# Moving operands laid out in eight places of a row and read in pieces of four, in a fused decoder layer

## The chip, the cores and the metric

The kernel runs on one core of one Trainium2 chip, in one launch. The metric is the device time of that core in microseconds, from the first to the last instruction of the execution; lower is better. Three runs of the kernel before gave 1671.35 to 1672.09 us, median 1671.76 us. Engines are named as the profile names them: PE (TensorE, products), PEld (its weight loads), DVE (VectorE), ACT (ScalarE), POOL (GpSimd) and SP (the queue that issues most transfers).

## The reference

One step of a hybrid decoder layer over 320 tokens: 256 prompt tokens and 8 sequences of 8 sample tokens, which share all weights. Everything is float32.

```
xn = rms_norm(x, g_mix);  z = xn @ w_in                    # 2048 -> 8704 columns
b, c, h, q, k, v, gate_c, gate_a = split(z)
y_conv = (b * conv3(c * h)) @ w_conv_out                   # causal, width 3
attn   = window_attend(q, k, v, bias, sinks)               # 16 heads, 4 kv heads, window 128
y_attn = attn @ w_attn_out
h1 = x + (sigmoid(gate_c)*y_conv + sigmoid(gate_a)*y_attn) @ w_o
h2 = h1 + (silu(n @ w_gate) * (n @ w_up)) @ w_down         # n = rms_norm(h1, g_ffn), 5632 wide
y  = rms_norm(h2, g_final)                                 # also new k, v and conv state
```

## The kernel before

Activations lie with features on the partitions and the 320 tokens (`T`) along the row, 16 rows of 128 features (`KC`). To keep float32 accuracy with the quick `float32r` product, every operand is split into a rounded part "hi" and a rest "lo", and each product is made three times: hi weights by hi tokens, hi weights by lo tokens, lo weights by hi tokens. The weights are the stationary operand (128x128); the tokens are the moving operand, one contiguous row of 320 elements, and they are written to the first 320 columns of a PSUM bank of 512.

`product` (lines 128 to 151) makes two output blocks of 128 columns at a time. `load_cols` (98) brings 4 rows of 256 weight columns (512 KB) by SP, ACT rounds them (`whi`, line 95), DVE subtracts (`wlo`, line 96), and 24 matmuls use them at line 142; a product over 2048 features has 96 matmuls. `passes` writes out the order: hi-hi and hi-lo of one place, with the lo-weight products three behind. `kv_product` (307) is the same with four blocks (line 331). The stages in time are `kv`; `q`; four rounds of `C`, `H`, `B` with the attention as side work between their products; eight rounds of `gc`, `ga`, `yc`, `ya`; eight of `wo`; and then twice the gate and up products (`fg`, `fu`) and the down product (`dn`), for 28 and for 16 of the 44 rows of the feed-forward width (`FH`).

Who writes the moving operands, each a hi tile and a lo tile with rows of 320: `x_prep` (272) the normed input, line 789 the convolution's output `cv`, `prompt_pv` (555) and line 690 the attention's output `at`, line 831 the merged `m`, line 849 the feed-forward input `hh`/`hl`. `q2` (444) lends rows of `at` to the queries before the attention's output is there.

`down` (874) differs. A row of `a_t` has 640 elements: hi of tokens 0 to 319, lo of tokens 128 to 319, lo of tokens 0 to 127. One matmul takes 512 of them at once with hi weights (line 898: all hi, and lo of the last 192 tokens), so that a full bank is written; a second (902) has the 128 lo elements as its stationary operand and 512 weight columns as the moving one; a third (906) is lo weights by the 320 hi elements. DVE adds the bank's two parts to `hT` (915, 916). The last 512 output columns (lines 1016 to 1092) hold their weights in spare room, use 384 columns at line 1045, 320 at 1049, and finish the first 128 tokens row by row at line 1083, where tokens are stationary.

Few lines carry the layout:

```
ps[c][:, :T], w[:, k, c * P:(c + 1) * P], x(kc),                                   # 143, moving operand x(kc)
ps[c], parts[k][0][:, cs], a_t[:, k, 0:512], start=k == 0, stop=False              # 899
last["hi"] = nc.scalar.activation(a_t[:, f, 0:T], gs[c], AF.Copy)                  # 955
for t0, t1, d0 in ((P, T, T), (0, P, 512)):                                        # 956, two subtractions
```

Of the kernel before, what the change touches and what calls it, by code (L numbers as in the profile page):

```python
# [38 lines left out]
TR = T - P  # L39
XB = [1] * 4 + [2] * 6  # L40
# [4 lines left out]
def hybrid_layer(ctx: ExitStack, tc: tile.TileContext, a: dict, o: list):  # L45
# [40 lines left out]
    def raw_tile():  # L86
        return wp.tile([P, KT, CW], F32, tag="wraw", name=u("wraw"), bufs=4)

# [39 lines left out]
    def product(load, nk, xh, xl, name, tiles=None, loaded=None):  # L128

        ps = [ps_acc(u(name)) for _ in range(2)]  # L130
        k0 = 0
        for n in tiles or [min(KT, nk - k) for k in range(0, nk, KT)]:
            hi, lo = load(k0, n)
            if loaded:
                loaded()
            order = [(k, c) for k in range(n) for c in range(2)]
            if k0 + n == nk:
                order.sort(key=lambda kc: kc[1])
            for k, c, i in passes(order, k0 + n == nk):
                kc = k0 + k  # L140
                w, x = ((hi, xh), (hi, xl), (lo, xh))[i]
                last["mm"] = nc.tensor.matmul(  # L142
                    ps[c][:, :T], w[:, k, c * P:(c + 1) * P], x(kc),
                    start=(kc == 0 and i == 0), stop=(kc == nk - 1 and i == 2),
                )
# [70 lines left out]
    xh_t = xp.tile([P, KC, T], F32R, tag="xh", name="xh_t")  # L216
    xl_t = xp.tile([P, KC, T], F32R, tag="xl", name="xl_t")
# [6 lines left out]

    def xh(kc):
        return xh_t[:, kc, :]

    def xl(kc):
        return xl_t[:, kc, :]
# [42 lines left out]
    def x_prep(kc):  # L272
        if kc == 0:
            m1 = nc.vector.tensor_scalar(xh_t[:, kc, :], hT[:, kc, :], g_mix[:, kc:kc + 1], None, op0=ALU.mult)
        else:
            m1 = nc.scalar.activation(xh_t[:, kc, :], hT[:, kc, :], AF.Copy, scale=g_mix[:, kc:kc + 1])
        m2 = nc.vector.scalar_tensor_tensor(
            xl_t[:, kc, :], hT[:, kc, :], g_mix[:, kc:kc + 1], xh_t[:, kc, :].bitcast(F32),
            op0=ALU.mult, op1=ALU.subtract,
        )  # L280
        mark[kc] = (m1, m2)
# [25 lines left out]
    def kv_product(tiles, x_after):  # L307

        ps = [ps_acc(u("kv")) for _ in range(4)]
        k0 = 0  # L310
        x_prep(0)
        for i, n in enumerate(tiles):
            hi, lo = load_kv(k0, n)
            if i == 0:
                x_prep(1)
            for b in x_after.get(i, ()):
                x_load(b)
            order = [(k, c) for k in range(n) for c in range(4)]
            if k0 + n == KC:
                order.sort(key=lambda kc: kc[1])  # L320
            seq = passes(order, k0 + n == KC)
            if i == 0:
                seq.sort(key=lambda kcm: kcm[2])
            for k, c, m in seq:
                kc = k0 + k
                if k0 and (k, c, m) == (0, 3 if n > 1 else 1, 0) and k0 + n < KC:
                    for kk in range(tiles[i + 1]):
                        x_prep(k0 + n + kk)
                    tick()
                w, x = ((hi, xh), (hi, xl), (lo, xh))[m]  # L330
                last["mm"] = nc.tensor.matmul(  # L331
                    ps[c][:, :T], w[:, k, c * P:(c + 1) * P], x(kc),
                    start=(kc == 0 and m == 0), stop=(kc == KC - 1 and m == 2),
                )
            k0 += n
            if i == 0:
                tick()
        return ps
# [4 lines left out]
    def small_loads():  # L343

        behind = nc.gpsimd.tensor_copy(gate, xh_t[:, 7, 0:1].bitcast(F32))
# [77 lines left out]
    cv_h = yy.tile([P, 8, T], F32R, name="cv_h")  # L423
    cv_l = yy.tile([P, 8, T], F32R, name="cv_l")
    at_h = yy.tile([P, 8, T], F32R, name="at_h")
    at_l = yy.tile([P, 8, T], F32R, name="at_l")
# [17 lines left out]
    def q2(ch, par):  # L444
        return (at_h, at_l)[par][:, ch, 0:TP]
# [109 lines left out]
    def prompt_pv(j, gp, pts):  # L555
        po = ps_aux(u("po"))
        steps = ((0, 0, 0, True, True), (1, 0, 1, True, False), (1, 1, 2, False, True))
        for b, t, kb, st_, sp_ in steps:
            for par in range(2):
                kv = j * 2 + par  # L560
                nc.tensor.matmul(
                    po[par * 64:(par + 1) * 64, b * 256:(b + 1) * 256],
                    vn[t][:, kv * HD:(kv + 1) * HD], pts[par][:, kb, :], start=st_, stop=sp_,
                )
        src = po.rearrange("p (b g q) -> p g b q", b=2, g=2)
        ch = j * 4 + gp * 2
        dh = at_h[:, ch:ch + 2, 0:TP].rearrange("p g (b q) -> p g b q", b=2)
        dl = at_l[:, ch:ch + 2, 0:TP].rearrange("p g (b q) -> p g b q", b=2)
# [28 lines left out]
    def sample_attention(sm):  # L597
# [92 lines left out]
        for j in range(2):  # L690
            src = pos[j][:, 0:256].rearrange("p (b g t) -> p g b t", b=NB, g=GRP)
            dh = at_h[:, j * 4:j * 4 + 4, TP:T].rearrange("p g (b t) -> p g b t", b=NB)
            dl = at_l[:, j * 4:j * 4 + 4, TP:T].rearrange("p g (b t) -> p g b t", b=NB)
            nc.scalar.activation(dh, src, AF.Copy)
            nc.vector.tensor_sub(dl, src, dh.bitcast(F32))
# [49 lines left out]
    for cp in range(4):  # L745
# [34 lines left out]
        for c in range(2):  # L780
# [8 lines left out]
            split_to(cv_h[:, ch, :], cv_l[:, ch, :], t[:, :T])  # L789
# [8 lines left out]
    m_h = mm.tile([P, KC, T], F32R, name="m_h")  # L798
    m_l = mm.tile([P, KC, T], F32R, name="m_l")
# [8 lines left out]
    for mp in range(8):  # L808
        c0 = mp * CW
        sg = {}  # L810
        for nm, off, tag in (("gc", O_GC, "ta"), ("ga", O_GA, "tb")):
# [8 lines left out]
            lambda k: cv_h[:, k, :], lambda k: cv_l[:, k, :], "yc",  # L820
        )
        for c in range(2):
            nc.vector.tensor_mul(sg["gc", c], ps[c][:, :T], sg["gc", c])
        ps = product(
            lambda k0, n: load_cols(w_ao, k0, n, c0), 8, lambda k: at_h[:, k, :], lambda k: at_l[:, k, :], "ya",
        )
        for c in range(2):
# [3 lines left out]
            split_to(m_h[:, mp * 2 + c, :], m_l[:, mp * 2 + c, :], t)  # L831
# [6 lines left out]
    hh_t = xp.tile([P, KC, T], F32R, tag="xh", name="hh_t")  # L838
    hl_t = xp.tile([P, KC, T], F32R, tag="xl", name="hl_t")
    for mp in range(8):  # L840
# [3 lines left out]
            lambda k: m_h[:, k, :], lambda k: m_l[:, k, :], "wo",  # L844
        )
        for c in range(2):
            k = mp * 2 + c
            nc.vector.tensor_add(hT[:, k, :], ps[c][:, :T], hT[:, k, :])
            nc.scalar.activation(hh_t[:, k, :], hT[:, k, :], AF.Copy, scale=g_ffn[:, k:k + 1])
            nc.vector.scalar_tensor_tensor(  # L850
                hl_t[:, k, :], hT[:, k, :], g_ffn[:, k:k + 1], hh_t[:, k, :].bitcast(F32),
# [18 lines left out]
    FH = (28, 16)  # L870

    ylow = op.tile([P, E0], F32, name="ylow")

    def down(half, c0):
# [6 lines left out]
        for i, k0s in enumerate(sets):  # L881
# [13 lines left out]
            for k, c, m in passes(order, end):  # L895
                cs = slice(c * P, (c + 1) * P)
                if m == 0:
                    nc.tensor.matmul(  # L898
                        ps[c], parts[k][0][:, cs], a_t[:, k, 0:512], start=k == 0, stop=False
                    )  # L900
                elif m == 1 and c == 0:
                    nc.tensor.matmul(  # L902
                        low, a_t[:, k, 512:], parts[k][0], start=k == 0, stop=k == nf - 1 and c0 < E0
                    )
                elif m == 2:
                    last["mm"] = nc.tensor.matmul(  # L906
                        ps[c][:, :T], parts[k][1][:, cs], a_t[:, k, 0:T], start=False, stop=k == nf - 1
# [5 lines left out]
        for c in range(4):  # L913
            k = c0 // P + c
            nc.vector.tensor_add(hT[:, k, :], hT[:, k, :], ps[c][:, :T])
            mark["out"].append(nc.vector.tensor_add(hT[:, k, P:T], hT[:, k, P:T], ps[c][:, T:]))
# [7 lines left out]
    for half in range(2):  # L924
        f0 = 0 if half == 0 else FH[0]
        nf = FH[half]

        a_big = fp.tile([P, FH[0], 2 * T], F32R, tag="at", name=u("a_t"))
        a_t = a_big[:, :nf, :]
        for fpair in range(nf // 2):  # L930
# [3 lines left out]
                lambda k: hh_t[:, k, :], lambda k: hl_t[:, k, :], "fg",  # L934
# [6 lines left out]
            for c in range(2):  # L941
# [8 lines left out]
                lambda k: hh_t[:, k, :], lambda k: hl_t[:, k, :], "fu",  # L950
            )
            for c in range(2):
                nc.vector.tensor_mul(gs[c], psu[c][:, :T], gs[c])
                f = fpair * 2 + c
                last["hi"] = nc.scalar.activation(a_t[:, f, 0:T], gs[c], AF.Copy)
# [61 lines left out]
    free = a_big[:, nf:, :].rearrange("p k t -> p (k t)")  # L1017
    more = xp.tile([P, 4 * KT * CW], F32R, tag="xl", name="more")
    for j in range(nf // 2):
        raw = wp.tile([P, 2, 512], F32, tag="wraw", name=u("wraw"), bufs=4)  # L1020
        nc.sync.dma_start(raw, w_d[E0 // 512, :, FH[0] + 2 * j:FH[0] + 2 * j + 2, :])
        if j < 5:
            src, n = (free, 2 * j) if j < 3 else (more, 2 * (j - 3))
            hi, lo = (
                src[:, i * KT * CW:(i + 1) * KT * CW].rearrange("p (k n) -> p k n", k=2) for i in (n, n + 1)
            )
# [10 lines left out]
    for i, ks in enumerate(sets):  # L1037
# [4 lines left out]
        for k, c, m in passes(order, end):  # L1042
            cs = slice(c * P, (c + 1) * P)
            if m == 0:
                nc.tensor.matmul(  # L1045
                    ps[c][:, P:512], held[k][0][:, cs], a_t[:, k, P:512], start=k == 0, stop=k == nf - 1
                )
            elif m == 2:
                last["mm"] = nc.tensor.matmul(
                    ps[c][:, :T], held[k][1][:, cs], a_t[:, k, 0:T], start=False, stop=k == nf - 1,  # L1050
                    skip_group_check=True,
# [9 lines left out]
    for c in range(4):  # L1061
        k = E0 // P + c
        rest = hT[:, k, P:T]
        with after(*(last[n] for n in ("lo", "out") if n in last)):
            nc.vector.tensor_add(rest, rest, ps[c][:, P:T])
            last["out"] = nc.vector.tensor_add(rest, rest, ps[c][:, T:512])
        sqs.append(rest_square(k))
        with after(last["out"]):
            if c:
                nc.vector.tensor_add(yacc, yacc, sqs[c - 1])  # L1070
            if c < 2:
                last["out"] = nc.vector.tensor_add(hT[:, k, 0:P], hT[:, k, 0:P], ps[c][:, 0:P])
    nc.vector.tensor_add(yacc, yacc, sqs[3])
    for c in (2, 3):
        k = E0 // P + c
        nc.vector.tensor_add(hT[:, k, 0:P], hT[:, k, 0:P], ps[c][:, 0:P])
# [3 lines left out]
    for k in range(nf):  # L1080
        (wh, wl), xhk, xlk = held[k], a_t[:, k, 0:P], a_t[:, k, 512:]
# [111 lines left out]
```

## Time and profile before

| | |
|---|---|
| median of three runs | 1671.76 us (1671.35 to 1672.09) |
| span of the profiled execution | 1669.8 us, 26302 instructions |
| PE busy | 1661.3 us, 10953 matmuls |
| DVE, ACT, POOL busy | 891.1, 647.2, 80.3 us |
| moved by the DMA engines | 258.13 MB, mean 155 GB/s |

The page prints the span and no other time of that execution; the median of the runs is 1.96 us above it. A row of a group reads: line, engine, operation, output<-inputs, shape, count, then busy time, mean of one in ns, and the idle time before them. The mean of one matmul there is its whole passage through the array; matmuls overlap, so what one costs is read from the distance between starts, that is from the chain of waits (start, length, what, count) or from a stretch with a known count.

### The profile page before, as it was taken

Reading aid. Unit: us, or ns where it says so; the run is one execution under the profiler, and the core shown is the slowest. Engines: PE = TensorE matmul, PEld = TensorE weight load, DVE = VectorE, ACT = ScalarE, POOL = GpSimd, SP = SyncE. Lnnn points to the kernel's source line nnn. Section 1 sums busy time; section 2 is a strip of 40 time slices with the busy share of each in tenths; the row PEclk is TensorE's granted clock in tenths of the full one; section 3 lists DMA queues with packets and bytes.
Section 4 is the critical chain, followed back from the end, with each engine's and each line's share of the span. In section 5 each row is a group of like instructions: output and inputs, shape, how many; then the busy total and the mean of one; then the engine's idle time right before and its main releaser. Section 6 shows DMA issues by size and latency. Waiting matters only on the chain.

```text
span 1669.8 us, 26302 instructions
## 1 busy us (share of the span) xinstructions
PE 1661.3 (99%) x10953; PEld 1618.1 (97%) x10953; DVE 891.1 (53%) x1284; ACT 647.2 (39%) x864; POOL 80.3 (5%) x123
## 2 busy tenths in 40 slices
PE   9999999999999999999999999999999999999998
PEld 9999999999999999999999999998888999999887
DVE  7778555444444445555555555553444455555556
ACT  7455433333333333344333333333333333333443
POOL 1101311000000002320000000000000000000000
PEclk9999999999999999999999999999999999999999
DMA  7554546544444444444444444445555444444552
GB/s 268 163 164 137 167 143 192 157 152 152 150 149 148 149 150 152 152 150 146 149 150 151 152 151 150 148 148 151 150 151 151 152 152 151 149 148 148 176 173 91
DMA packets 74399, 258.13 MB, mean 155 GB/s; under 512 B 8552, under 2 KB 11928, under 8 KB 74152
## 3 DMA queue, kind: packets, MB, share of 16 engines
q1 hardware_dynamic: 71880, 249.86, 48.2%
q0 software_dynamic: 1968, 5.90, 1.2%
q8 instruction: 86, 1.41, 0.4%
q10 hardware_dynamic: 432, 0.69, 0.1%
q14 instruction: 33, 0.27, 0.0%
HBM read 253.30 MB, written 5.08 MB: 155 GB/s over the span
## 4 chain that ended last, share of the span: by engine, by line
PE 99%; DMA 0%; DVE 0%; ACT 0%; DVEq 0%; SPq 0%; issue 0%
PE fg L142 19%; PE fu L142 19%; PE dn L898 9%; PE ga L142 7%; PE wo L142 7%; PE gc L142 7%; PE dn L906 6%; PE B L142 3%; PE C L142 3%; PE q L142 3%; PE yc L142 3%; PE ya L142 3%; PE H L142 3%; PE dl L902 2%; PE kv L331 2%; PE dn L1045 1%
## 5 line engine op out<-in xcount | busy, mean ns | idle before, releaser
L96 DVE TENSOR_TENSOR wlo<-wraw,whi 128x1024 fp32r<-128x1024 f32 (+1 forms) x461 | 562.7, 1221 | 640.5 <-ACT whi L95 633.7
L95 ACT ACTIVATE whi<-wraw 128x1024 fp32r<-128x1024 f32 (+1 forms) x461 | 486.0, 1056 | 783.3 <-PE dn L898 157.7
L898 PE MATMUL dn<-a_t,whi 128*128 128x512 f32 x640 | 218.8, 394 | 0.0
L142 PE MATMUL fg<-hh_t,whi 128*128 128x320 f32 x704 | 212.4, 309 | 0.0
L142 PE MATMUL fu<-hh_t,whi 128*128 128x320 f32 x704 | 212.4, 309 | 0.0
L142 PE MATMUL fg<-hl_t,whi 128*128 128x320 f32 x704 | 212.3, 309 | 0.0
L142 PE MATMUL fu<-hl_t,whi 128*128 128x320 f32 x704 | 212.3, 309 | 0.0
L142 PE MATMUL fg<-hh_t,wlo 128*128 128x320 f32 x704 | 164.0, 309 | 0.0
L142 PE MATMUL fu<-hh_t,wlo 128*128 128x320 f32 x704 | 164.0, 309 | 0.0
L906 PE MATMUL dn<-a_t,wlo 128*128 128x320 f32 x640 | 152.1, 309 | 0.0
L898 PEld LDWEIGHTS dn<-a_t,whi 128*128 128x128 f32 x640 | 119.3, 188 | 23.5
L142 PEld LDWEIGHTS fg<-hh_t,whi 128*128 128x128 f32 x704 | 132.2, 188 | 0.0
L142 PEld LDWEIGHTS fu<-hh_t,whi 128*128 128x128 f32 x704 | 132.2, 188 | 0.0
L142 PEld LDWEIGHTS fu<-hl_t,whi 128*128 128x128 f32 x704 | 132.2, 188 | 0.0
L142 PEld LDWEIGHTS fg<-hl_t,whi 128*128 128x128 f32 x704 | 132.2, 188 | 0.0
L906 PEld LDWEIGHTS dn<-a_t,wlo 128*128 128x128 f32 x640 | 112.4, 188 | 10.9
L142 PEld LDWEIGHTS fg<-hh_t,wlo 128*128 128x128 f32 x704 | 118.6, 188 | 0.0
L142 PEld LDWEIGHTS fu<-hh_t,wlo 128*128 128x128 f32 x704 | 118.6, 188 | 0.0
L142 PE MATMUL ga<-xh_t,whi 128*128 128x320 f32 x256 | 77.3, 310 | 0.0
L142 PE MATMUL gc<-xh_t,whi 128*128 128x320 f32 x256 | 77.3, 310 | 0.0
L142 PE MATMUL ga<-xl_t,whi 128*128 128x320 f32 x256 | 77.3, 310 | 0.0
L142 PE MATMUL gc<-xl_t,whi 128*128 128x320 f32 x256 | 77.3, 310 | 0.0
(310 smaller groups left out, 2736.6 us busy)
## 6 DMA issues: line engine op xcount, KB each, us to landing
wraw<-in_w_in_dram SPq DMA_DIRECT2D x128, 512.0 KB, 3.8
wraw<-in_w_gate_dram SPq DMA_DIRECT2D x88, 512.0 KB, 3.8
wraw<-in_w_up_dram SPq DMA_DIRECT2D x88, 512.0 KB, 3.7
wraw<-in_w_down_dram SPq DMA_DIRECT2D x88, 512.0 KB, 3.7
wraw<-in_w_o_dram SPq DMA_DIRECT2D x32, 512.0 KB, 3.8
wraw<-in_w_conv_out_dram SPq DMA_DIRECT2D x16, 512.0 KB, 3.7
wraw<-in_w_attn_out_dram SPq DMA_DIRECT2D x16, 512.0 KB, 3.7
wraw<-in_w_kv_dram SPq DMA_DIRECT2D x6, 512.0 KB, 6.9
```

The lines of the kernel that those rows point to most:

```text
L95: last["hi"] = nc.scalar.activation(hi, src, AF.Copy)
L96: last["lo"] = nc.vector.tensor_sub(lo, src, hi.bitcast(F32))
L142: last["mm"] = nc.tensor.matmul(ps[c][:, :T], w[:, k, c * P:(c + 1) * P], x(kc), start=(kc == 0 and i == 0), stop=(kc == nk - 1 and i == 2),)
L331: last["mm"] = nc.tensor.matmul(ps[c][:, :T], w[:, k, c * P:(c + 1) * P], x(kc), start=(kc == 0 and m == 0), stop=(kc == KC - 1 and m == 2),)
L898: nc.tensor.matmul(ps[c], parts[k][0][:, cs], a_t[:, k, 0:512], start=k == 0, stop=False)
L902: nc.tensor.matmul(low, a_t[:, k, 512:], parts[k][0], start=k == 0, stop=k == nf - 1 and c0 < E0)
L906: last["mm"] = nc.tensor.matmul(ps[c][:, :T], parts[k][1][:, cs], a_t[:, k, 0:T], start=False, stop=k == nf - 1)
L1045: nc.tensor.matmul(ps[c][:, P:512], held[k][0][:, cs], a_t[:, k, P:512], start=k == 0, stop=k == nf - 1)
```

## The change

A row of a moving operand now holds hi and lo together: eight places, each with the hi part of 40 consecutive tokens and then the lo part of the same 40 (80 elements, 320 bytes). `placed` views a row as 8 places, `turns` views it as a loop over (group of 4, place, element of 4): a matmul reads 4 elements of place 0, 4 of place 1, and so on to place 7, then the next 4 of place 0. The output is written with the same view of the bank, 4 columns at a stride of 40, so that in `product` token t stays in column t. The number of columns of every product is unchanged.

In the feed-forward, `a_rows` lays the eight places far apart: each place holds 64 elements of every row of a group (16 hi of the first 128 tokens, 24 hi and 24 lo of the other 192), with 16 elements of room between places, so 3648 bytes from place to place in the first half and 2112 in the second. The lo part of the first 128 tokens lies by itself, and in the second half also a plain copy of their hi part, for the products where tokens are stationary. DVE's addition of a bank to `hT` takes three instructions instead of two, the rounding two instead of one, and the attention's output is written in more pieces.

```diff
+def placed(ap):
+    return ap.rearrange("p (s j) -> p s j", s=NP)
+def turns(ap):
+    return ap.rearrange("p s (i b) -> p i s b", b=4)
+def halves(name):
+    return [xp.tile([P, KC // 2, 2 * T], F32R, tag=t, name=f"{name}_{t}") for t in ("xh", "xl")]
+def operand(*tiles):
+    n = tiles[0].shape[1]
+    def part(a):
+        return lambda k: placed(tiles[k // n][:, k % n, :])[:, :, a:a + JT]
+    return part(0), part(JT)
...
-                    ps[c][:, :T], w[:, k, c * P:(c + 1) * P], x(kc),
+                    turns(placed(ps[c][:, :T])), w[:, k, c * P:(c + 1) * P], turns(x(kc)),
...
-        dh = at_h[:, ch:ch + 2, 0:TP].rearrange("p g (b q) -> p g b q", b=2)
-        dl = at_l[:, ch:ch + 2, 0:TP].rearrange("p g (b q) -> p g b q", b=2)
-        nc.scalar.activation(dh, src, AF.Copy)
-        nc.vector.tensor_sub(dl, src, dh.bitcast(F32))
+        for g in range(2):
+            row, part = placed(rows[:, g])[:, :whole], src[:, g, 0:n].rearrange("p (s j) -> p s j", j=JT)
+            two_to(row[:, :, 0:JT], row[:, :, JT:], part)
+        w0 = whole * 2 * JT
+        two_to(rows[:, :, w0:w0 + TP - n], rows[:, :, w0 + JT:w0 + JT + TP - n], src[:, :, n:])
...
+    def a_rows(half):
+        nf = FH[half]
+        per = nf // 2
+        step = per * JM + 16
+        flat = fp.tile([P, A_ALL], F32R, tag="at", name=u("a_t"))
+        ends = [2 * NP * step + i * nf * P for i in range(3)]
+        def move(k):
+            g = k // per * NP * step
+            return placed(flat[:, g:g + NP * step])[:, :, k % per * JM:(k % per + 1) * JM]
+        low, first = (lambda k, e=e: flat[:, e + k * P:e + (k + 1) * P] for e in ends[:2])
+        return move, low, first, flat[:, ends[2]:] if half else None
...
-                        ps[c], parts[k][0][:, cs], a_t[:, k, 0:512], start=k == 0, stop=False
+                        turns(placed(ps[c])), parts[k][0][:, cs], turns(a_move(k)), start=k == 0, stop=False
...
-            nc.vector.tensor_add(hT[:, k, :], hT[:, k, :], ps[c][:, :T])
-            mark["out"].append(nc.vector.tensor_add(hT[:, k, P:T], hT[:, k, P:T], ps[c][:, T:]))
+            got, (first, rest) = placed(ps[c]), h_parts(k)
+            nc.vector.tensor_add(first, first, got[:, :, 0:JR])
+            nc.vector.tensor_add(rest, rest, got[:, :, JR:JT])
+            mark["out"].append(nc.vector.tensor_add(rest, rest, got[:, :, JT:]))
...
-                last["hi"] = nc.scalar.activation(a_t[:, f, 0:T], gs[c], AF.Copy)
-                for t0, t1, d0 in ((P, T, T), (0, P, 512)):
-                    last["lo"] = nc.vector.tensor_sub(
-                        a_t[:, f, d0:d0 + t1 - t0], gs[c][:, t0:t1], a_t[:, f, t0:t1].bitcast(F32)
-                    )
+                (first, rest), row = parts_of(gs[c]), a_move(f)
+                nc.scalar.activation(row[:, :, JR:JT], rest, AF.Copy)
+                last["hi"] = nc.scalar.activation(row[:, :, 0:JR], first, AF.Copy)
+                nc.vector.tensor_sub(row[:, :, JT:], rest, row[:, :, JR:JT].bitcast(F32))
+                last["lo"] = nc.vector.tensor_sub(placed(a_low(f)), first, row[:, :, 0:JR].bitcast(F32))
+                if half == 1:
+                    nc.scalar.activation(a_first(f), gs[c][:, 0:P], AF.Copy)
```

Here `NP` is 8, `JT` = 40, `JR` = 16 and `JM` = 64. Lines 906, 1045 and 1049 get the same views as lines 143 and 899; line 902 and line 1083 keep contiguous operands. The order of the matmuls on PE is the same but for six exchanges of neighbours at lines 1045 and 1049, and the issues of SP and POOL are the same.

More of the change, by code (lines that the diff above doesn't have):

```diff
@@ L422, in hybrid_layer @@
     yy = yp.enter_context(tc.tile_pool(name="yy", bufs=1))
[L423 to L426, printed above, removed]
+    cv_t = yy.tile([P, 8, 2 * T], F32R, name="cv_t")
+    at_t = yy.tile([P, 8, 2 * T], F32R, name="at_t")
+    cv_h, cv_l = operand(cv_t)
+    at_h, at_l = operand(at_t)
     g18 = yy.tile([P, 8, 2 + 2 * NB], F32, name="g18")
@@ L926, in hybrid_layer @@
         nf = FH[half]
[L928 to L929 removed]
+        a_move, a_low, a_first, free = a_rows(half)
         for fpair in range(nf // 2):
@@ L1016, in hybrid_layer @@
     held = []
-    free = a_big[:, nf:, :].rearrange("p k t -> p (k t)")
-    more = xp.tile([P, 4 * KT * CW], F32R, tag="xl", name="more")
+    more = xp.tile([P, 5 * KT * CW], F32R, tag="xl", name="more")
+    blocks = [t[:, i * KT * CW:(i + 1) * KT * CW].rearrange("p (k n) -> p k n", k=2) for t in (free, more) for i in range(5)]
     for j in range(nf // 2):
@@ L1022, in hybrid_layer @@
         if j < 5:
[L1023 to L1026, printed above, removed]
+            hi, lo = blocks[2 * j:2 * j + 2]
         else:
```

99 lines of the change are left out of this document (57 added, 42 removed).

## The prediction

> **What bounds the kernel now.** I read the page's busy shares first, then its chain of waits, then stretches of known content.
>
> ```profile
> span 1669.8 us, 26302 instructions
> ...
> PE 1661.3 (99%) x10953; PEld 1618.1 (97%) x10953; DVE 891.1 (53%) x1284; ACT 647.2 (39%) x864; POOL 80.3 (5%) x123
> ...
> PEclk9999999999999999999999999999999999999999
> ...
> PE 99%; DMA 0%; DVE 0%; ACT 0%; DVEq 0%; SPq 0%; issue 0%
> ```
>
> PE is busy in 99% of the span and 99% of the chain that ended last is PE; the clock is granted throughout. So only two things can move the time: what one matmul costs, and a new wait of PE. The cost of one is read from the distance of starts, in the chain (start, length, what, count):
>
> ```profile
> 110.57 0.24 PE ps L501 x2
> 110.80 0.12 PE ps L504
> ...
> 1113.07 14.08 PE fu L142 x96
> ...
> 1322.87 14.09 PE fg L142 x96
> ...
> 1648.80 0.70 PE dn L1045 x4
> ```
>
> 14.08 us for 96 matmuls of 320 columns is 146.7 ns each. Is that the array's own pace, or does something hold it back? Busy and quiet stretches tell:
>
> ```profile
> core 0: us, PE busy (x) PEld busy (x) DVE busy (x) ACT busy (x) POOL busy (x), PEclk, DMA share, GB/s
> ...
> 5.08:33.22 28.14, 28.14 (x192) 28.14 (x193) 26.10 (x48) 24.39 (x49) 3.84 (x7) 1.00 0.87 311
> 1127.15:1322.87 195.72, 195.72 (x1011) 170.77 (x1010) 80.18 (x88) 60.72 (x61) 0.00 (x0) 1.00 0.51 150
> 1322.87:1548.16 225.29, 225.29 (x1537) 225.29 (x1537) 116.89 (x160) 84.44 (x99) 0.00 (x0) 1.00 0.49 150
> ```
>
> The first stretch (`kv`) has DVE at 93%, ACT at 87%, the DMA engines at 0.87, and 28.14 / 192 = 146.6 ns a matmul. The third (`fg`, `fu`) has DVE at 52%, the DMA at 0.49, and 225.29 / 1537 = 146.6 ns. Traffic of the other engines doesn't change the pace, nor do other rows of the operands. The second stretch is the down product of the first half: 28 rows by 4 chunks give 448 matmuls at line 898 and 112 at 902 of 512 columns, and 448 at 906 of 320. (195.72 - 448 x 0.1467) / 560 = 0.2322 us for 512 columns. From 320 to 512 columns is 85.5 ns, 0.445 ns per column, and 146.7 - 320 x 0.445 leaves 4.2 ns that don't grow with the columns. This line gives 175 ns for 384 columns (the chain: 0.70 / 4 = 175) and 118 for 256 (the chain: 0.24 / 2 = 120). So the cost is one price per column plus 4 ns.
>
> Is 0.445 ns the array's step? The one other row of pure streaming is the warm-up, bf16 ones read and written contiguously; beside it stands the end of the span, after PE's last work:
>
> ```profile
> L270 PE MATMUL wm<-const-bfloat16-1.0 128*128 128x256 bf16 x15 | 3.4, 418 | 0.8 <-PEq L1176 0.8
> ```
>
> ```profile
> 1666.00:1669.80 3.80, 0.00 (x0) 0.00 (x0) 0.00 (x0) 0.00 (x0) 0.00 (x0) 0.55 0.53 209
> ```
>
> Fourteen starts in 3.4 - 0.418 = 2.98 us are 213 ns for 256 columns, 0.832 ns each. An idle PE falls to about half its clock (0.55 as a mean of the last 3.8 us), and the warm-up follows idleness, so I read its 0.832 as the half clock and 0.416 ns as a column's step at the full one: an estimate. Then 0.445 - 0.416 = **0.029 ns per column is a surplus**: 9.4 ns of a 320-column matmul, 15.0 of 512, 11.3 of 384. It grows with the columns, appears in every product alike, and isn't traffic. What a float32r column has that the warm-up's hasn't is twice the bytes to read, from consecutive addresses. That is what the change alters.
>
> **The change part by part.** Matmuls whose moving operand and output are now taken in turn:
>
> ```profile
> L142 PE MATMUL fg<-hh_t,whi 128*128 128x320 f32 x704 | 212.4, 309 | 0.0
> L142 PE MATMUL ga<-xh_t,whi 128*128 128x320 f32 x256 | 77.3, 310 | 0.0
> L142 PE MATMUL q<-xh_t,whi 128*128 128x320 f32 x128 | 38.7, 310 | 0.0
> L331 PE MATMUL kv<-xh_t,whi 128*128 128x320 f32 x64 | 19.2, 313 | 0.1
> L898 PE MATMUL dn<-a_t,whi 128*128 128x512 f32 x640 | 218.8, 394 | 0.0
> L906 PE MATMUL dn<-a_t,wlo 128*128 128x320 f32 x640 | 152.1, 309 | 0.0
> ```
>
> Each product has three such groups. `fg` and `fu`: 6 x 704; `gc`, `ga`, `wo`: 9 x 256; `q`, `C`, `H`, `B`, `yc`, `ya`: 18 x 128; `kv`: 3 x 64; line 906: 640; line 1049: 16 rows by 4 blocks, 64. Together 9664 + 64 = 9728 of 320 columns; 640 of 512; 64 of 384 (line 1045). Lines 902 and 1083 keep their contiguous operands.
>
> What does a turn cost or save? No row of before has it. From below: all of the surplus goes, 9728 x 9.4 + 640 x 15.0 + 64 x 11.3 ns = 91.4 + 9.6 + 0.7 = **101.7 us saved**. In the middle: nothing changes. From above: every piece of 4 costs a step more, since it begins at another place; 80 pieces by 0.416 ns are 33.3 ns, less the 9.4 ns they would replace, so +23.9 ns a matmul; 512 columns have 128 pieces, +38.3 ns; 384 have 96, +28.6 ns: 232.5 + 24.5 + 1.8 = **258.8 us lost**. The nearest row is line 504, whose moving operand comes in two pieces 1024 bytes apart: 0.12 us against 0.24 / 2 for the contiguous ones of line 501. One leap is lost in the rounding, but two rounded numbers can't exclude a few ns. I take the gain: the surplus needs a cause that is the same in all stretches and proportional to the columns, and the sequence of addresses is the one such thing in sight. In turn, neighbouring reads lie 320, 3648 or 2112 bytes apart, all eight different, instead of 16 bytes apart, so whatever part of the memory serves one read is not asked again at once.
>
> Beside PE, these are added:
>
> ```profile
> L760 DVE TENSOR_TENSOR ue<-H,csb 128x256 f32<-128x256 f32 x8 | 3.3, 418 | 0.0
> L761 DVE TENSOR_TENSOR ue<-H,csb 128x64 f32<-128x64 f32 x8 | 1.7, 215 | 0.0
> ...
> L915 DVE TENSOR_TENSOR xv<-xv,dn 128x320 f32<-128x320 f32 x28 | 13.6, 487 | 15.7 <-PE dn L906 15.7
> L916 DVE TENSOR_TENSOR xv<-xv,dn 128x192 f32<-128x192 f32 x28 | 9.9, 352 | 0.8
> L1072 DVE TENSOR_TENSOR xv<-xv,dn 128x128 f32<-128x128 f32 x2 | 0.6, 281 | 0.0
> L570 DVE TENSOR_TENSOR at_l<-po,at_h 128x512 fp32r<-128x512 f32 x4 | 2.7, 685 | 0.5 <-ACT at_h L569 0.5
> ```
>
> ```profile
> L955 ACT ACTIVATE a_t<-gs 128x320 fp32r<-128x320 f32 x44 | 20.8, 472 | 39.8 <-DVE gs L953 39.8
> L985 ACT ACTIVATE sq<-xv 128x192 f32<-128x192 f32 x15 | 5.3, 358 | 14.8 <-DVE xv L1066 7.5 <-DVE xv L916 4.2 <-DVE yacc L997 3.1
> L569 ACT ACTIVATE at_h<-po 128x512 fp32r<-128x512 f32 x4 | 2.4, 593 | 1.8 <-PE po L561 1.7
> L694 ACT ACTIVATE at_h<-spo 128x256 fp32r<-128x256 f32 x2 | 0.7, 380 | 2.1 <-PE spo L684 2.1
> ```
>
> Line 761 handles pieces of 8 elements and costs 215 ns for 64, line 760 418 for 256 in one piece: 1.06 ns an element and some 148 ns of start, with no sign of a price per piece. So pieces of 16, 24 and 40 cost what their elements cost, and only starts are added. DVE: a bank's addition becomes 281 + 352 + 352 for 487 + 352, 146 ns by 28, 4.1 us; the attention's `po` some 0.37 us by 4, 1.5 us. ACT: 358 and about 300 for 472, by 44, 8.2 us; the copy of the first 128 tokens 16 x 0.3 = 4.8 us; `po` 1.5 us. That is about 6 us on DVE and 15 on ACT, hidden behind 779 and 1023 us of idleness: a row of `a_t` made last is used last in the down product, some 45 us on, a row of `m` at the fourth weight tile, 10 us on. Uncovered, they would cost their 6 and 15 us. I charge 4 us for what is exposed where a stage hands its last rows to the next.
>
> A quicker PE asks its suppliers for more.
>
> ```profile
> wraw<-in_w_gate_dram SPq DMA_DIRECT2D x88, 512.0 KB, 3.8
> ```
>
> ```profile
> SPq L100 <- DVE wlo L96: 1126.5, 359, 10.5
> ```
>
> SP waits for a buffer, not the buffers for SP, with four of them and 3.8 us to land; a tile would be used up in 24 x 137.3 = 3.30 instead of 3.52 us. Only `kv`, where DVE needs 26.10 of 28.14 us and the DMA engines 0.87, can't give its 1.8 us safely, and I leave them out. Sum: 1671.8 - 101.7 + 1.8 + 4 = **1576 us** (the profiled execution's span, 1669.8, with the 2.0 us around it, is the median of the runs).
>
> **The rivals.** *Slower by the pieces:* each begins with a step of its own, for the read or for the write of the bank, and from 9.4 / 80 = 0.12 ns a piece on the change loses; at one step a piece 1671.8 + 258.8 + 4 = 1935 us. For it: the surplus itself could be a price of passing from one stretch of memory to the next, which pieces would multiply. Against it: line 504. [...]
>
> *No change on PE:* the surplus belongs to float32r or to the array, whatever the addresses; PE keeps 146.7 ns and the time is 1672 to 1676 us. For it: the pace is exactly the same for operands of every tile. [...]
>
> *A wait instead:* PE unchanged and the added work of DVE and ACT uncovered, 1671.8 + 6 + 15 = 1693 us at most. Hi and lo lying in one row could also tie an early read to a late write. Against it: both engines are idle half the time, and PE's order is the same.
>
> **How the numbers follow.** Gain on PE 0.68, no change on PE 0.08, a wait or a small loss on PE 0.06, a price per piece 0.18. The gain's own range is 1554 (the surplus and half of the 4.2 ns per matmul gone, 22 us more) to 1627 (half of the surplus left). The range that leaves out the price per piece and little else is 1554 to 1700. A measurement of this kernel tells no change from 0.2%, 3.3 us: faster 0.68, the same 0.08, slower 0.24.
>
> **What would show it.** Right: `fg` and `fu` take 13.2 us per 96 matmuls in the chain instead of 14.08, `kv` 137 to 140 ns a matmul, the 512-column ones 217, lines 902 and 1083 unchanged, PE still 99%. Wrong: 14.08 us again (inherent), 16 us or more (a price per piece), or a chain with DVE or ACT above 1% (a wait).

## The result, and the profile after

| | median, us | from, to | runs |
|---|---|---|---|
| before | 1671.59 | 1671.35, 1672.09 | 4 |
| after | 1622.87 | 1621.95, 1623.06 | 4 |

The ratio is 0.9707, with an interval of 0.9694 to 0.9721: the change saves 48.7 us, half of the 95.8 us forecast. The profiled executions differ by 1669.8 - 1621.4 = 48.4 us. From the page of after, the span, the busy times and the shares of the chain:

```profile
span 1621.4 us, 26411 instructions
...
PE 1612.6 (99%) x10953; PEld 1573.2 (97%) x10953; DVE 887.2 (55%) x1322; ACT 652.5 (40%) x934; POOL 79.8 (5%) x123
...
PE 99%; DVE 1%; ACT 0%; issue 0%; DVEq 0%
```

PE has as many matmuls as before and ends last almost everywhere, so the time came out of the single matmul. The chain of waits of after (start, length, what, count):

```profile
4.95 28.16 PE kv L349 x192
...
44.71 1.16 DVE wlo L120
...
301.95 6.85 PE yc L166 x48
...
601.94 109.26 PE wo L166 x768
...
1078.90 13.61 PE fu L166 x96
...
1608.21 5.60 PE rowacc L1135 x24
```

`fu` takes 13.61 us for 96 (`fg`, `gc` and `ga` too), 141.8 ns each instead of 146.7; `yc` 142.7; `wo` 142.3. Line 1135 is line 1083 of before, which was not altered: 5.60 us for 24, 5.62 before. Between 44.05 and 56.81 us, in `q`, the chain now runs through DVE and ACT, where before it ran through PE. PE lost at most 0.33 us there (below); the kernel "rows in place", which adds no work to DVE, has the same row there (43.73 us, `wlo`), so the added instructions are not its cause.

`kv` as a whole keeps its 28.16 us, but not its pace. Its first matmuls, from the timeline of after (start, length, what, count):

```profile
4.71 2.32 PE L349 MATMUL kv<-x_xh,whi 128*128 128x320 f32 x8
6.87 0.73 PE L349 MATMUL kv<-x_xh,wlo 128*128 128x320 f32 x4
7.44 0.74 PE L349 MATMUL kv<-x_xh,whi 128*128 128x320 f32 x4
```

The first eight start (6.87 - 4.71) / 8 = 270 ns apart on average, about the warm-up's pace for 320 columns (320 x 0.832 = 266 ns), and the next four (7.44 - 6.87) / 4 = 143 ns apart. From the 13th matmul to the last, the starts lie 141.8 ns apart in after and 146.7 in before. So `kv` gained its 4.9 ns a matmul too, and lost most of that to a slow start of PE. In before, the first four started at 4.45, 4.68, 5.08 (after a wait for `whi`) and 5.33 us and the fifth at 5.48: only the steps of 230 and 250 ns were that slow, and the next was 150. The kernel without the room (below), whose `kv` is the same, took 27.71 us, so this start differs from one execution to the next. The clock rows do not show it: they have 1.00 there.

By stage, first the stretches of after (us, then busy time and count of PE, PEld, DVE, ACT, POOL, the granted clock, the DMA share, GB/s), then the two of before that the prediction does not show, and the last one:

```profile
33.11:711.21 678.10, 677.77 (x4898) 673.47 (x4897) 386.73 (x594) 277.71 (x417) 70.54 (x104) 1.00 0.51 160
711.21:1092.51 381.30, 381.30 (x2691) 381.30 (x2691) 205.89 (x286) 150.60 (x200) 3.42 (x3) 1.00 0.49 155
1092.51:1284.28 191.77, 191.77 (x1011) 169.22 (x1010) 81.18 (x103) 60.78 (x62) 0.00 (x0) 1.00 0.52 154
1284.28:1501.99 217.71, 217.71 (x1537) 217.71 (x1537) 115.98 (x161) 87.83 (x129) 0.57 (x1) 1.00 0.50 160
1501.99:1621.40 119.41, 111.81 (x610) 100.22 (x609) 69.87 (x126) 48.70 (x78) 0.00 (x0) 0.98 0.46 141
```

```profile
33.22:732.62 699.40, 699.40 (x4898) 695.05 (x4897) 389.88 (x584) 277.72 (x407) 70.83 (x104) 1.00 0.50 155
732.62:1127.15 394.53, 394.53 (x2692) 394.53 (x2691) 207.59 (x286) 148.81 (x173) 3.41 (x3) 1.00 0.48 150
1548.16:1669.80 121.64, 114.04 (x610) 101.34 (x609) 69.08 (x114) 48.61 (x76) 0.57 (x1) 0.99 0.46 147
```

| stage | before, us | after, us | saved, us |
|---|---|---|---|
| `q` to `wo`, attention between | 699.40 | 678.10 | 21.30 |
| `fg`, `fu`, first half | 394.53 | 381.30 | 13.23 |
| down product, first half | 195.72 | 191.77 | 3.95 |
| `fg`, `fu`, second half | 225.29 | 217.71 | 7.58 |
| down product, second half, and the end | 121.64 | 119.41 | 2.23 |

Together 48.29 us, the whole difference but 0.1 us. The gain is spread nearly evenly over what the change touches, 4.9 ns a matmul in `fg` and `fu` ((14.08 - 13.61) / 96); what is missing is missing there too. Beside PE little stands in the way: PE is idle for 678.10 - 677.77 = 0.33 us in the first stretch, and for 7.60 us in the last one, as before (121.64 - 114.04). The added instructions cost what the prediction gave them (from the groups of after: line, engine, operation, count, busy time, mean in ns, idle time before):

```profile
L1008 ACT ACTIVATE a_t<-gs 128x128 fp32r<-128x128 f32 x44 | 13.0, 295 | 0.0
...
L966 DVE TENSOR_TENSOR xv<-xv,dn 128x128 f32<-128x128 f32 x28 | 8.0, 286 | 13.5 <-PE dn L955 13.5
```

The addition's 286 ns were foreseen as 281, the ACT copy's 295 as about 300.

### The profile page after: what moved, and what is told of

It reads as the page before. It is cut to its first block, busy times and chain, and to the rows that moved or that the text cites. A ratio compares the mean times of both kernels' runs of the same rounds, so it can differ in the third digit from the quotient of the medians.

```text
span 1621.4 us, 26411 instructions
## 1 busy us (share of the span) xinstructions
PE 1612.6 (99%) x10953; PEld 1573.2 (97%) x10953; DVE 887.2 (55%) x1322; ACT 652.5 (40%) x934; POOL 79.8 (5%) x123
## 3 DMA queue, kind: packets, MB, share of 16 engines
HBM read 253.30 MB, written 5.08 MB: 159 GB/s over the span
## 4 chain that ended last, share of the span: by engine, by line
PE 99%; DVE 1%; ACT 0%; issue 0%; DVEq 0%
PE fg L166 18%; PE fu L166 18%; PE dn L947 9%; PE wo L166 7%; PE ga L166 7%; PE gc L166 7%; PE dn L955 6%; PE B L166 3%; PE yc L166 3%; PE ya L166 3%; PE C L166 3%; PE H L166 3%; PE q L166 3%; PE dl L951 2%; PE kv L349 2%; PE dn L1095 1%
## 5 line engine op out<-in xcount | busy, mean ns | idle before, releaser
L166 PE MATMUL fg<-h_xh,whi 128*128 128x320 f32 x704 | 131.9, 303 | 0.0
L166 PE MATMUL fu<-h_xh,whi 128*128 128x320 f32 x704 | 131.9, 303 | 0.0
L166 PE MATMUL fg<-h_xl,whi 128*128 128x320 f32 x704 | 122.9, 303 | 0.0
L166 PE MATMUL fu<-h_xl,whi 128*128 128x320 f32 x704 | 122.9, 303 | 0.0
L166 PEld LDWEIGHTS fg<-h_xh,whi 128*128 128x128 f32 x704 | 110.0, 188 | 0.0
L166 PEld LDWEIGHTS fu<-h_xh,whi 128*128 128x128 f32 x704 | 110.0, 188 | 0.0
L166 PEld LDWEIGHTS fu<-h_xl,whi 128*128 128x128 f32 x704 | 107.3, 188 | 0.0
L166 PEld LDWEIGHTS fg<-h_xl,whi 128*128 128x128 f32 x704 | 107.3, 188 | 0.0
L166 PE MATMUL wo<-m_t,whi 128*128 128x320 f32 x512 | 92.9, 304 | 0.0
L166 PE MATMUL fg<-h_xh,wlo 128*128 128x320 f32 x352 | 85.6, 304 | 0.0
```

Source lines behind the costliest of these rows:

```text
L166: last["mm"] = nc.tensor.matmul(turns(placed(ps[c][:, :T])), w[:, k, c * P:(c + 1) * P], turns(x(kc)), start=(kc == 0 and i == 0), stop=(k ...
```

## The experiments

**The pace by itself.** Is it the read or the write that gains, and does it depend on the distance of the places? One kernel runs blocks of 96 matmuls of 320 columns on PE with every other engine idle. `run` takes a name, the view that is read and the view that is written; `turn(placed(...))` is the read of after, `o_cont` a bank written in order, `step160_` has its places 40 elements apart, and `far(step, 8, 4)` reads pieces of 4 from 8 places at a distance of `step` elements:

```diff
+    run("turn_", lambda k, m: turn(placed(k, m)), lambda ps: turn(o_rows(ps)))
+    run("onlyread_", lambda k, m: turn(placed(k, m)), o_cont)
+    run("onlywrite_", lambda k, m: cont(k, m).rearrange("p (i s b) -> p i s b", s=8, b=4), lambda ps: turn(o_rows(ps)))
+    run("step160_", lambda k, m: turn(rows(k, m)), lambda ps: turn(o_rows(ps)))
+    run("by2_", lambda k, m: turn(placed(k, m), 2), lambda ps: turn(o_rows(ps), 2))
+    for step in (64, 72, 80, 96, 112, 128, 144, 256, 272, 512, 912, 1024):
+        run(f"s{step}_", far(step, 8, 4), o_cont)
+    run("same_", lambda k, m: X[:, 0:4].unsqueeze(1).to_broadcast([P, 80, 4]), o_cont)
+    run("one_w_", cont, o_cont, w=lambda k, c, m: W[:, 0:P])
```

> The kernel computes nothing of the layer: it holds only blocks of 96 matmuls (320 columns, the order of one product of 2048 features), one block for each way of reading and writing, with nothing else running beside them; a block of the kernel before took 14.08 us, one of the changed kernel 13.61. Theory A (the price sits in reading consecutive addresses): the block that only reads in turn takes 13.6, the one that only writes the bank in turn 14.08, and the distance between places matters little as long as it is not small. Theory B (the price sits in the bank): the other way round. Theory C (the moving read and the load of the next weights meet in the same part of the memory): reading in turn takes between 13.3 and 14.1 depending on the distance of the places (odd multiples of 64 bytes, that is steps of 80, 112, 144, 272 and 912 elements, quick; 64, 96, 128, 256, 512, 1024 no better than 14.08), and with one and the same weight block for every matmul the pace changes. Theory D (float32r itself): the block that reads the same four elements again and again keeps 14.08 and bf16 takes less. Under A and C that block takes 13.2 or less.

Its chain of waits ("again" is the plain row, at the end):

```profile
55.76 13.74 PE turn L98 x96
69.50 13.71 PE onlyread L98 x96
83.20 14.08 PE onlywrite L98 x96
97.28 14.72 PE step L98 x96
...
390.63 13.31 PE same L98 x96
403.94 14.08 PE one_w L98 x96
...
444.80 14.08 PE again L98 x96
```

The read alone gains all (13.71 us) and the write alone nothing (14.08, like the plain row): theory B falls. The plain row takes 14.08 us with every other engine idle, as in the layer. With no reading of new addresses at all, the same 4 elements again and again, 96 matmuls take 13.31 us, a little more than the 13.2 that theories A and C gave it; theory D, which kept it at 14.08, falls. One weight tile for all matmuls changes nothing (`one_w`), so the part of theory C that has the weights meet the read falls too; what it says of the distances holds (below) but for 112 elements, which it called quick (14.07 us). Against the same 4 elements a plain row costs (14.08 - 13.31) / 96 = 8.0 ns more, and the turn of this change takes (14.08 - 13.74) / 96 = 3.5 ns of it; the second kernel of PE alone, below, has blocks that are quicker still. Why the same view takes 13.74 here and 13.61 in the layer is open. With places 40 elements apart it loses instead. As stretches of this kernel, first the block with pieces of 2 in place of 4, then blocks with other distances, 8 places each: 64, 80, 96 and 912 elements (a count of 97 or 98 takes in a neighbour at the edge):

```profile
139.99:166.48 26.49, 26.49 (x97) 19.86 (x97) 0.00 (x0) 0.00 (x0) 0.00 (x0) 1.00 0.00 1
...
166.48:183.27 16.79, 16.79 (x98) 16.79 (x98) 0.00 (x0) 0.00 (x0) 0.00 (x0) 1.00 0.00 1
...
197.40:211.17 13.77, 13.77 (x98) 13.77 (x98) 0.00 (x0) 0.00 (x0) 0.00 (x0) 1.00 0.00 1
211.17:225.71 14.54, 14.54 (x98) 14.54 (x98) 0.00 (x0) 0.00 (x0) 0.00 (x0) 1.00 0.00 1
...
317.77:331.56 13.79, 13.79 (x98) 13.79 (x98) 0.00 (x0) 0.00 (x0) 0.00 (x0) 1.00 0.01 1
```

With eight places and pieces of 4, the blocks order themselves by the distance in bytes modulo 256; only the classes 0 and 64 have more than one distance:

| distance in bytes, modulo 256 | elements tried | us per 96 |
|---|---|---|
| 0 | 64, 128, 256, 512, 1024 | 16.78 to 16.82 |
| 32 | 72 | 14.13 |
| 64 | 80, 144, 272, 912 | 13.77 to 13.79 |
| 128 | 96 | 14.54 |
| 160 | 40 (the block "step") | 14.72 |
| 192 | 112 | 14.07 |

All three distances of after, 320, 3648 and 2112 bytes, are 64 modulo 256. That is where its gain comes from, not from the turn as such. Pieces of 2 at the same 320 bytes, read and also written so, take 26.49 us; pieces of 8, read and written so, take 13.88.

**The view alone, in the layer.** Before, with its contiguous rows, reads and writes in the order of after: eight places of 40 elements, 160 bytes apart.

```diff
+    def turns(ap):
+        return ap.rearrange("p (s i b) -> p i s b", s=8, b=4)
-                    ps[c][:, :T], w[:, k, c * P:(c + 1) * P], x(kc),
+                    turns(ps[c][:, :T]), w[:, k, c * P:(c + 1) * P], turns(x(kc)),
```

(lines 143 and 332; the down product is that of before)

> Only the two matmul lines of the kernel before read their rows, and write their bank, in eight places of 40 and pieces of 4; the rows stay contiguous, so the places are 160 bytes apart, and the down product is as before. Theory A: the products of 320 columns fall from 14.08 to about 13.6 us per 96 and the time to about 1628 us. Theory C (a distance of 160 bytes brings two places into the same 64 bytes): little or no gain, 1660 to 1672 us, or a loss.

1731.49 us (1731.12 to 1731.86), ratio 1.0358 with an interval of 1.0328 to 1.0388: 60 us slower. Its chain:

```profile
1593.85 14.72 PE fu L145 x96
```

14.72 us, exactly the block "step" above: theory A falls, and theory C, which allowed for a loss, gave no size for it. Whoever had kept the rows and changed the views alone would have reported a loss.

**No room between the places.** After, without the 16 elements of room that `a_rows` puts between the places of the down product: 3584 and 2048 bytes from place to place, 0 modulo 256. Nothing else differs.

```diff
-        step = per * JM + 16
+        step = per * JM
```

> The changed kernel without the 16 elements of room between the places of the feed-forward rows, so that they lie 3584 and 2048 bytes apart, multiples of 256, instead of 3648 and 2112. Theory C1: the down product takes the pace of 16.8 us per 96, that is 0.175 us for 320 columns and about 0.277 for 512, against 0.142 and 0.228: 640 x 0.049 + 704 x 0.033 + 64 x 0.04 = 57 us more, about 1680 us, and nothing else changes. Theory A (any distance will do): 1623 us.

1681.46 us (1681.1 to 1681.83), ratio to before 1.0058 with an interval of 1.0038 to 1.0078. The first half's down product, and one row of the unchanged products:

```profile
1092.06:1321.64 229.58, 229.58 (x1011) 185.92 (x1010) 81.39 (x103) 62.98 (x62) 0.00 (x0) 1.00 0.44 128
```

```profile
1078.45 13.61 PE fu L166 x96
```

The down product takes 229.58 us instead of 191.77, at 13.61 us per 96 elsewhere. Those 64 bytes of room are worth 58.6 us, more than the whole change gains. 37.81 us over 448 pairs of one matmul of 512 and one of 320 columns are 84.4 ns a pair; a pair has 128 + 80 = 208 pieces, so 0.41 ns a piece more than in after. The forecast of theory C1 (places fall into four groups of 64 bytes that take turns every 256 bytes; set out with the next run), 57 us more, holds in the layer.

**What the surplus is made of.** A second kernel of PE alone: other lengths, other orders. `pat(n, step, 4)` reads a contiguous row in turn from n places `step` elements apart, `ap` a view of its own, and `o_n` gives the columns written.

```diff
+    run("turn_sixteen", pat(20, 16, 4), o_cont)
+    run("turn_thirtytwo", pat(10, 32, 4), o_cont)
+    run("turn_sixtyfour", pat(5, 64, 4), o_cont)
...
+        run(f"rowturn_{'abcd'[base // 4]}", lambda k, m, b=base: ap(b, (4, 4), (16, 20), (1, 4)), o_cont)
...
+        run(f"again_{dict([(8, 'eight'), (16, 'sixteen'), (32, 'thirtytwo'), (64, 'sixtyfour')])[n]}", lambda k, m, n=n: ap(0, (0, T // n), (1, n)), o_cont)
...
+    run("wide_plain", lambda k, m: ap(k * 640, (1, 512)), o_n(512))
+    run("wide_same", lambda k, m: ap(0, (0, 128), (1, 4)), o_n(512))
+    run("narrow_plain", lambda k, m: ap(k * 640, (1, 256)), o_n(256))
+    run("narrow_same", lambda k, m: ap(0, (0, 64), (1, 4)), o_n(256))
...
+    run("two_sixteen", lambda k, m: ap(k * 640, (4, 40), (16, 2), (1, 4)), o_cont)
...
+    run("four_sixteen", lambda k, m: ap(k * 640, (4, 20), (16, 4), (1, 4)), o_cont)
```

> Blocks of 96 matmuls alone again, nothing of the layer. In the first such kernel a block of 320 columns took 14.08 us in plain order, 13.7 with places 80, 144, 272 or 912 elements apart, 14.7 with 40, 16.8 with 64, 128, 256, 512 or 1024, and 13.31 when the same four elements were read again and again. Theory C1 (four groups of 64 bytes each that take turns every 256 bytes; a read is slowed when it opens another 64 bytes of the group that was just used): twenty places 16 elements apart inside the contiguous row, with no new layout, take about 13.7 us; 32 apart (two groups) about 14.5; 64 apart (one group) 16.8. Theory C2 (the far distance itself matters, as in the changed layout): 16 apart is no better than 14.08. For both: 16 elements read again and again cost 13.3, as four do; if 32 or 64 elements read again cost 14.08, the price is one for each 64 bytes opened. For 512 columns in turn: under C1 about 0.224 us each against 0.232. One weight column for all: no change against plain, 14.08, if the weights play no part.

```profile
69.26 13.45 PE turn_sixteen L98 x96
82.71 15.35 PE turn_thirtytwo L98 x96
98.07 16.00 PE turn_sixtyfour L98 x96
...
197.35 13.12 PE rowturn_c L98 x96
...
251.41 14.55 PE again_sixteen L98 x96
...
308.21 21.83 PE wide_plain L98 x96
...
351.49 20.99 PE wide_same L98 x96
372.48 11.52 PE narrow_plain L98 x96
...
395.16 10.75 PE narrow_same L98 x96
...
420.63 14.72 PE two_sixteen L98 x96
...
448.80 13.70 PE four_sixteen L98 x96
```

A plain row less the same 4 elements is 0.77 / 96 = 8.0 ns for 256 columns, 8.0 for 320 and 0.84 / 96 = 8.8 for 512: this difference belongs to the matmul, not to its columns. The same 4 elements take 112.0 ns for 256 columns and 218.6 for 512, which is 0.4167 ns per column and 5.3 ns. They are not the quickest read, though: a row of 320 read in turn from 32 bytes beyond a multiple of 64, counted from the start of its tile (`rowturn_c`), takes 13.12 us, and the bf16 block of the first such kernel took 13.06. Up to (14.08 - 13.12) / 96 = 10.0 ns of a plain matmul of 320 columns can go.

And a contiguous row can be read in turn where it lies: 64 bytes from place to place takes 13.45 us, better than the eight places of this change. Two things limit this: with only two places 64 bytes apart the block loses (14.72 us; four take 13.70), and pieces of 8 at 64 bytes gain nothing (14.09). So the distance alone does not decide. Theory C2 falls with the 13.45. Theory C1 has the order of the distances and not the sizes: 15.35 us for 14.5 at 128 bytes, 16.00 for 16.8 at 256, 14.55 for 13.3 with 16 elements again. A price for each newly opened stretch of 64 bytes, one theory of that run, does not hold: 16 elements read over and over open nothing and take more than a plain row.

**Rows in place, in the layer.** Before, with its rows and all its other instructions as they are; only the views of the matmuls (lines 143, 332, 899, 907, 1046, 1050) differ.

```diff
+    def turns(ap):
+        return ap.rearrange("p (s i b) -> p i s b", i=4, b=4)
-                    ps[c][:, :T], w[:, k, c * P:(c + 1) * P], x(kc),
+                    turns(ps[c][:, :T]), w[:, k, c * P:(c + 1) * P], turns(x(kc)),
```

> The kernel before with its contiguous rows; only the matmul lines read them, and write the bank, in pieces of 4 from places 16 elements (64 bytes) apart: 20 places of a row of 320, 32 of 512, 24 of 384. Nothing is added on DVE or ACT. Theory C1: the pace of the changed kernel without its layout, 13.6 to 13.7 us per 96 matmuls and 1617 to 1625 us in all. Theory C2: 14.08 or slower, 1672 us or more.

1609.24 us (1607.73 to 1609.95), ratio 0.9627 with an interval of 0.9611 to 0.9643: 62.5 us less than before and 13.6 less than after, without a new layout. From its page and its chain:

```profile
span 1606.0 us, 26302 instructions
```

```profile
1055.74 13.44 PE fg L145 x96
```

13.44 us for 96 are 140.0 ns, 1.8 ns less than after, and the spans differ by 1621.4 - 1606.0 = 15.4 us. By stretches, 11.7 us of this lie in the products outside `kv` and the down product, 0.9 in `kv` (27.25 us) and 2.9 in the down product and the end. In those products 1.8 ns for each of the 8832 matmuls would be 15.6 us; but half of the rounds of `gc` and `ga` took 13.72 to 13.74 us with the same operands, and no run says why. The time is also below the 1617 to 1625 us that theory C1 gave it. So the wider layout, its 109 added instructions and the room in the rows are not needed for the gain.

**Why 512 columns cost 232 ns in the layer.** Alone a plain one takes 21.83 us per 96, 227.4 ns, but the prediction's row of the down product gave 232.2. A third kernel of PE alone shifts the first element of the row.

```diff
+    for off, n in ((0, "zero"), (8, "eight"), (4, "four")):
+        run(f"wide_{n}", lambda k, m, o=off: plain(o)(k, 512), o_n(512))
+        run(f"wideturn_{n}", lambda k, m, o=off: turned(o)(k, 512), o_n(512))
+        run(f"rows_{n}", lambda k, m, o=off: plain(o)(k, 320), o_cont)
+        run(f"rowsturn_{n}", lambda k, m, o=off: turned(o)(k, 320), o_cont)
+    for off, n in ((0, "zero"), (8, "eight")):
+        mix(f"mix_{n}", plain(off), plain(off))
+        mix(f"mixturn_{n}", turned(off), turned(off))
```

> Computes nothing of the layer: blocks of 96 matmuls, PE alone, of 512 columns (wide) and of 320 (rows), plain or in turn (pieces of 4, places 16 elements apart), with the row's first element at 0, 8 (32 bytes) or 4 (16 bytes) beyond a multiple of 64 bytes; then 48 of 512 and 48 of 320 columns mixed four by four in the order of the down product. The question is why a plain matmul of 512 columns costs 232 ns in the layer and 227.4 alone. Theory O, the place of a_t's row (32 bytes beyond a multiple of 64): wide_eight plain 22.29 us per 96, wide_zero 21.83; mix_zero 48 x (227.4 + 146.7) = 17.96 us, mix_eight 18.18. Theory M, the change between 512 and 320 columns: wide_zero and wide_eight both 21.83, both mixes plain 18.2 or more. Theory N, neither (something of the layer beside PE): all at 21.83, 14.08 and 17.96. Turned: 21.46 (wide), 13.45 (rows), 17.46 (mix) under N; under O the turned ones at 8 lose what the plain ones lose.

```profile
69.44 21.79 PE wide_zero L98 x96
...
126.77 13.49 PE rowsturn_zero L98 x96
140.26 22.40 PE wide_eight L98 x96
...
184.32 14.09 PE rows_eight L98 x96
198.41 13.12 PE rowsturn_eight L98 x96
...
283.18 18.12 PE mix_zero L127 x96
301.31 18.12 PE mixturn_zero L127 x96
319.43 18.24 PE mix_eight L127 x96
337.67 17.34 PE mixturn_eight L127 x96
```

At 32 bytes beyond a multiple of 64 a plain matmul of 512 columns takes 22.40 us per 96, 233.3 ns, and one of 320 the same 14.09 as elsewhere: that much is theory O. That `a_t` lies so in the kernel before was worked out from the tiles ahead of it; no trace shows an address. But mixing sizes costs too, as theory M had it. With 146.7 ns for a matmul of 320 columns, one of 512 costs 18.12 / 48 - 0.1467 = 0.2308 us in the mix where the place is good, and 18.24 / 48 - 0.1467 = 0.2333 at 32 bytes. The layer's 232.2 ns lie between them, so this run does not part the place from the mix.

Theory O failed where it had the turned blocks lose at 32 bytes what the plain ones lose. Those of 512 columns lose some (21.67 us for 21.46), but those of 320 gain (13.12 for 13.49), and in the mix the turn takes 0.90 us off (17.34 for 18.24), while at the good place it gains nothing there, which no theory named.

## Why the direction held and half the gain was missing

- *The bound.* Right: PE sets the end but for 0.33 us, a plain matmul's pace is independent of traffic (14.08 us per 96 in the layer and alone), and a shorter one is saved in full. The sum by stages leaves 0.1 us over.
- *The step of a column, 0.416 ns from the half-clock warm-up.* Right in size: the same 4 elements take 0.4167 ns per column over 256 to 512 columns, and plain rows of 256 and 320 differ by the same (14.08 - 11.52) / 96 / 64 = 0.4167. The half clock itself was assumed: the clock rows of before have 1.00 from 0 to 5.08 us, and also from 1662 to 1666 us, where PE has 0.20 us of work; the 0.55 belongs to the last 3.8 us alone.
- *"0.029 ns per column is a surplus", growing with the columns.* Wrong, the first step that failed. The line was drawn through 320 and 512 columns, and the 512-column ones of the down product pay some 5 ns that others do not (232.2 ns for 21.83 / 96 = 227.4 alone), for their place, for the mix of sizes or both. Against the same 4 elements the surplus is 8 to 9 ns a matmul at 256, 320 and 512 columns alike. Its size for 320 columns, 9.4 ns, lies between these 8.0 and the 10.0 of the quickest block, so the size was not what failed; its cause as a price per column was.
- *"All of the surplus goes."* Wrong, and the larger part. The turn of this layout takes 4.8 ns a matmul in the layer: 42.1 us measured over `q` to `wo` and both halves of `fg` and `fu`, for 8832 x 9.4 ns = 83.0 forecast. The argument, that a neighbouring read need only lie elsewhere, has no distance in it, and distance matters: 160 bytes lost 60 us. The forecast had no row for this and took the bound from below as its value. That all three distances of the change lie in the quick class was no part of the argument, so that there was a gain at all was in this respect luck.
- *The down product.* Forecast 704 x 9.4 ns + 9.6 + 0.7 = 16.9 us, measured 3.95 + 2.23 = 6.2: the same two terms, mis-sized. By the distances of starts in the first half's traces, 512 columns went from 232.5 to 227.5 ns (15.0 ns forecast) and 320 from 146.9 to 142.6.
- *`kv` left out.* The number was right, 28.16 us against 28.14, and the reason was not: DVE and the DMA engines did not hold it. Its matmuls took the quicker pace, and a slow start of the first eight ate most of the gain; the kernel with its rows in place did `kv` in 27.25 us.
- *Exposed work of DVE and ACT, 4 us.* Too much: 0.33 us of idle PE. The durations shown were right, and so was the cover.
- *The price per piece.* Refuted for this layout, and yet a loss of about its size was paid elsewhere: at multiples of 256 bytes a matmul of 320 columns takes (16.79 - 14.08) / 96 = 28.2 ns more than a plain row, where the rival had 23.9. Its reason, that each piece begins at another place, is not shown by this, since pieces at 64 bytes begin so too and gain (13.45 us per 96). Nor did the write of the bank take a step a piece: written in turn and read in order, 96 matmuls took 14.08 us, as the plain row does.
- *No change on PE.* Refuted by the 4.9 ns, and its "whatever the addresses" by the blocks with eight places and pieces of 4, which took 13.77 to 16.82 us by the distance alone.
- *A wait instead.* Refuted: the chain has DVE at 1% and ACT at 0%, and the DVE pieces in it cost at most 0.33 us.
- *The signs.* `fg` and `fu` at 13.2 us were named, 13.61 came; 217 ns for 512 columns, and with line 902 taken as unchanged (191.77 - 448 x 0.1418 - 112 x 0.2322) / 448 = 228 came. No sign was named for a part of the gain.

Open is the mechanism. The distance modulo 256 bytes, the number of places, the length of a piece and the first element's place all matter, but no run says why 64 is better than 192, why 16 elements repeated are slow, or why the turn gains nothing in the mix at offset 0. Nor was a row order tried in the layer with `a_t` moved to a multiple of 64 bytes.

## What to carry to other kernels

When PE is busy to the end, compare the pace of a matmul with that of other reads of the same length (the same few elements again, a row in turn) before looking for waits; here 8 to 10 ns of 147 lay between them, and a view alone won 6.7. The order in which the moving operand is read is a free choice of the view, if the output's view matches: in these runs pieces of 4 float32r elements from four or more places 64 bytes apart (modulo 256) gained in blocks of 320 columns (13.12 to 13.79 us per 96 for 14.08), two places (14.72) and pieces of 8 at 64 bytes (14.09) did not, and multiples of 256 bytes lost most (16.00 to 16.82). A layout whose places lie a multiple of 64 elements apart falls into the slow case by itself, as the kernel without the room did (58.6 us), and a line drawn through two tiles measures their places and their neighbours too (232.2 ns for 512 columns in the down product, 227.4 alone).

## What the hardware showed unexpectedly

- With eight places and pieces of 4 elements, the distance of the places moves a 320-column float32r matmul from 143.4 ns (13.77 us / 96, at 64 modulo 256 bytes) to 175 ns (16.79 / 96, at 0).
- Neither one weight tile for all (14.08 us per 96) nor a bank written in turn (14.08) moves the pace.
- Reading the same 16 elements repeatedly (14.55 us per 96) is slower than reading 320 different ones (14.08); reading the same 4 takes 13.31, and 320 different ones in turn from a place 32 bytes beyond a multiple of 64 only 13.12.
- A first element 32 bytes beyond a multiple of 64, counted from the start of the tile, slows 512 columns in plain order (22.40 us against 21.79), leaves 320 in plain order alone (14.09 against 14.08), and speeds up 320 in turn (13.12 against 13.49).
- After the warm-up the first eight matmuls of `kv` started 270 ns apart on average and the next four 143, with the clock rows at 1.00 throughout.
